# Decoder layer on one core: the feed-forward's block sums reordered, its down sums kept in PSUM, its first loads thinned, its operand stores begun by ScalarE

## The chip, the cores and the metric

One Trainium2 chip, one of its cores. The metric is device time of one execution in microseconds; the kernel before is given by the median of three runs.

## The reference

One decoder layer on a sequence of 1024 tokens of width 1024, all in 32-bit floats, cut to what matters here:

```
mod = silu(c) @ w_ada + b_ada                  # six vectors of 1024: sh1, sc1, g1, sh2, sc2, g2
h   = x * (1 + sc1) + sh1
y   = mixers(h @ w_in) @ w_o                   # sparse attention (8 heads) and gated MLP (8 groups)
x   = LN(alpha * x + (1 + g1) * y)
h   = x * (1 + sc2) + sh2
f   = (silu(h @ w1) * (h @ w3)) @ w2           # w1, w3: 1024 x 2816, w2: 2816 x 1024
out = LN(alpha * x + (1 + g2) * f)
```

## The kernel before

All matrix products of the large projections are made from split operands: a 32-bit value a becomes aH (rounded to the engine's fp32r form by ScalarE, `rnd` at L102) and aL = a − aH (by VectorE, `sub` at L107), and a product is three matmuls, HH, HL and LH, summed in PSUM. So TensorE's work needs, for every operand, one ScalarE and one VectorE operation ahead of it (`split`, L179).

The order of work on each engine comes from a list scheduler that simulates the program's time while it is built; the order in the source is the priority, and `order(a, b)` adds an edge that orders a after b without a semaphore. Tiles come from pools with a fixed number of buffers: `B` (41 of 128x1024), `RAW` (4 of 128x1024, where loads land), `H2` (4 of 128x512; with the tag "pt" another 6), and in PSUM `G` (3 banks), `OT` (1 bank) and `S2` (2 pairs of banks). Every transfer of the kernel before is started by SyncE, whose queue takes them in order.

*Start.* c is loaded as a row copied to 128 partitions (`crow`), goes through tanh to silu(c), and `mod_col` (L156) sums each row of the transposed w_ada against it. `make_h` (L228) makes the split h of a 128-row block k from x and mod; `split_start` (L197) splits the v and k weights of two blocks; `start_mm` multiplies. The loads stand in one written order (`dseq`): crow, cols, v weights, then per block the modulation weights and x.

*Turn to the feed-forward.* After the output projection (`out_proj`) VectorE makes the layer norm Z of 8 row tiles; the last ones end with L990. `make_h2a` transposes rows 512 to 1023 of Z on TensorE and makes the split h operands B11 and B21, `make_h2b` those of rows 0 to 511: B22 and the sums T1 to T4.

*Up.* The two up products (w = 0 is w1 with silu, w = 1 is w3) and the down product each use a block scheme with seven products of half-size blocks instead of eight (the Strassen-Winograd form), so every operand of it is a block or a sum of blocks. A step (p, w) covers 256 columns of the weights; there are 22. `prep1` loads and splits A11 and A12, `prep2` makes the sums S1 to S4 and A22. `up_first`, `up_second` and `up_rest` multiply (`prod`, 12 matmuls each), copy and add the seven products, and `act_out` makes silu and the product. Each block and each sum of blocks that the down product needs is stored to DRAM by `put` (L1001) at once: seven of the activations and seven of w2 for each p (`w2_sums`, scaled by g2 on POOL at L1011). The first NE = 4 steps' `up_first` and `up_second`, which need B11 and B21 alone, run while `make_h2b` works.

*Down.* For each of seven products P1 to P7 (order `DN`) and 11 blocks p, `prep_down` loads a stored operand pair (cr), splits it, and `down` makes 12 matmuls, four row tiles t by three. P1 to P7 are added to the residual rows R on VectorE (`add`, L1168), P1 and P5 by way of copies (`sn`) on ScalarE. Small pieces of work wait in `todo` and are taken one per product by `step()`. The last LAST = 6 blocks of P4 are taken row tile by row tile; after each t its layer norm follows, in `norm_slow` (VectorE, ScalarE, POOL) for t = 0 and 1, in `norm_fast` (VectorE) for t = 2 and 3.

Of the kernel before, what the change touches and what calls it, by code (L numbers as in the profile page):

```python
# [19 lines left out]
NK = 8  # L20
# [15 lines left out]
W1 = 768  # L36
# [7 lines left out]
def hymba_kernel(ctx, tc, x, c, w_ada, b_ada, w_in, cmp_pos, cmp_w1, cmp_w2, vn_g, vn_b, w_s, b_s,  # L44
# [88 lines left out]
    def dseq(o, i):  # L133
        d = dma(o, i)
        if seq[0] is not None:
# [4 lines left out]
    dseq(crow, c[0:1].to_broadcast([128, 1024]))  # L140
# [56 lines left out]
    def split_start(k2):  # L197
        h, l, t = B("wH", F32R), B("wL", F32R), B("wK", F32R)
        chain("A", A_.activation(h, wvr[k2], AF.Copy))
        chain("A", A_.activation(t[:, 0:512], wkr[k2], AF.Copy))  # L200
        chain("V", sub(l, wvr[k2], h))
        chain("V", sub(t[:, 512:1024], wkr[k2], t[:, 0:512]))
        for i in range(2):
            wv.append((h[:, i * 512:(i + 1) * 512], l[:, i * 512:(i + 1) * 512]))
# [89 lines left out]
    for k in range(NK):  # L294
        for j in (1, 0):
            chain("V", mod_col(j, j, k, adat[j, k]))
        if k == 0:
            split_start(0)
        if k % 2 and k < 7:
            split_start(k // 2 + 1)  # L300
        make_h(k, 0, 512, W1)
# [519 lines left out]
    X1, BOP = [None] * NK, {n: [None] * 4 for n in ("B11", "B21", "B22", "T1", "T2", "T3", "T4")}  # L821
# [14 lines left out]
    def make_h2a():  # L836

        for k in range(NK):
            if k % 2 == 0:
                bh, bl, bx = B("h2H", F32R), B("h2L", F32R), B("h2X")  # L840
            h, l, xx = halves(bh)[k % 2], halves(bl)[k % 2], halves(bx)[k % 2]
# [5 lines left out]
            X1[k] = xx  # L847
# [4 lines left out]
    def make_h2b():  # L852

        for i in range(4):
            if i % 2 == 0:
                bh, bl = B("h2H", F32R), B("h2L", F32R)
            xs = []
            for k in (i, 4 + i):
                p = S2("pz")[:, 0, :]
                trans4(p, lambda j: Z[j][:, k * 128:(k + 1) * 128])  # L860
                xx = H2(F32, "pt")
                affine("A", xx, p, k)
                xs.append(xx)
                if k >= 4:
                    h, l = halves(bh)[i % 2], halves(bl)[i % 2]
                    affine("A", h, p, k)
                    sub(l, xx, h)
                    BOP["B22"][i] = (h, l)
            ta, tb = B("ta"), B("tb")
            (t1, t3), (t2, t4) = halves(ta), halves(tb)  # L870
            V_.tensor_tensor(t1, xs[0], X1[i], SUB)
            V_.tensor_tensor(t3, xs[1], xs[0], SUB)
            V_.tensor_tensor(t2, xs[1], t1, SUB)
            V_.tensor_tensor(t4, X1[4 + i], t2, SUB)
            for t, (n0, n1) in ((tb, ("T2", "T4")), (ta, ("T1", "T3"))):
                h, l = split(t)
                for n, hh, ll in zip((n0, n1), halves(h), halves(l)):
                    BOP[n][i] = (hh, ll)
            yield
        spill_z(0)  # L880

# [86 lines left out]
    for n_, (ts, chunks) in enumerate(groups):  # L968
# [13 lines left out]
        for t, o in zip(ts, os_):  # L982
# [7 lines left out]
            V_.tensor_scalar(z, z, mv[:, 0:1], mv[:, 2:3], SUB, MULT)  # L990
# [7 lines left out]
    DN = ("P1", "P5", "P2", "P3", "P6", "P7", "P4")  # L998
    comb = {(i, p): dram.tile([128, 1024], F32, name=f"comb{i}_{p}") for i in DN for p in range(NP)}

    def put(i, p, side, src):  # L1001

        dma(comb[i, p][:, side * 512:side * 512 + 512], src)

    def w2_sums(p):
        (b11, b12), (b21, b22) = r = [halves(RAW("w2r")) for _ in range(2)]
        for z in range(2):
            load(r[z][0], w2[(2 * p + z) * 128:(2 * p + z + 1) * 128, 0:512], 8)
            load(r[z][1], w2[(2 * p + z) * 128:(2 * p + z + 1) * 128, 512:1024], 8)
            for a in range(2):  # L1010
                P_.tensor_tensor(r[z][a], r[z][a], rowt["g2r"][:, a * 512:a * 512 + 512], MULT)  # L1011
# [27 lines left out]
    def prep2(p, w):  # L1039
# [6 lines left out]
        V_.tensor_tensor(s1, a21, a22, ADD)  # L1046
# [312 lines left out]
```

## Time and profile before

| | |
|---|---|
| runs | 1258.51 us median of 3 (1256.99 to 1259.09) |
| the profiled execution's own time | 1261.56 us |
| its span, first to last instruction | 1259.8 us |
| busy: TensorE, VectorE, ScalarE, POOL | 95%, 77%, 46%, 28% |
| mean granted clock of TensorE | 0.988 |
| DMA, mean | 150 GB/s, 188.59 MB |

Times in the profile count from the first instruction. PE is TensorE, PEld its weight loads, DVE VectorE, ACT ScalarE, POOL GpSimd, SP or SPq SyncE and its queue. A matmul's busy time is longer than its place in a full pipeline, so for the pace of TensorE the reader counts matmuls in a stretch. The idle time before an instruction is given with what ended it. Names are those of the program's tiles without their numbers; combP is the DRAM buffer of the down operands.

### The profile page before, as it was taken

Reading aid. Unit: us, or ns where it says so; the run is one execution under the profiler, and the core shown is the slowest. Engines: PE = TensorE matmul, PEld = TensorE weight load, DVE = VectorE, ACT = ScalarE, POOL = GpSimd, SP = SyncE. Lnnn points to the kernel's source line nnn. Section 1 sums busy time; section 2 is a strip of 40 time slices with the busy share of each in tenths; the row PEclk is TensorE's granted clock in tenths of the full one; section 3 lists DMA queues with packets and bytes.
Section 4 is the critical chain, followed back from the end, with each engine's and each line's share of the span. In section 5 each row is a group of like instructions: output and inputs, shape, how many; then the busy total and the mean of one; then the engine's idle time right before and its main releaser. Section 6 shows DMA issues by size and latency. Waiting matters only on the chain. (4 is left out here: it accounts for less than half of the span.)

```text
span 1259.8 us, 16940 instructions
## 1 busy us (share of the span) xinstructions
PE 1196.9 (95%) x5880; PEld 994.4 (79%) x5880; DVE 964.6 (77%) x1686; ACT 581.2 (46%) x1065; POOL 355.8 (28%) x357
## 2 busy tenths in 40 slices
PE   5999999999999999998899999999999989999994
PEld 4888888788888888887678777888878868888873
DVE  6568798699999998778858668666686758784587
ACT  5653223499889994134433232332333325454131
POOL 0022035166456753103133222332313310000123
PEclk9999999999999999999999999999999999999997
DMA  9623549110000006634245555556555479686252
GB/s 353 250 61 120 162 127 246 45 68 1 2 1 2 2 18 219 200 113 147 84 141 188 175 172 176 176 161 198 181 179 181 161 264 331 220 300 213 77 191 83
DMA packets 131225, 188.59 MB, mean 150 GB/s; under 512 B 16834, under 2 KB 77378, under 8 KB 131140
## 3 DMA queue, kind: packets, MB, share of 16 engines
q1 hardware_dynamic: 131140, 187.52, 45.6%
q8 instruction: 46, 0.75, 0.3%
q14 instruction: 39, 0.32, 0.1%
HBM read 136.63 MB, written 48.76 MB: 147 GB/s over the span
## 5 line engine op out<-in xcount | busy, mean ns | idle before, releaser
L730 POOL TENSOR_SCALAR P<-P,ast,gate 128x640 f32<-128x640 f32 (+7 forms) x128 | 99.6, 784 | 66.7 <-DVE ast L729 49.7
L107 DVE TENSOR_TENSOR wL<-cr,wH 128x1024 fp32r<-128x1024 f32 x77 | 99.9, 1317 | 22.9 <-ACT wH L102 22.4
L102 ACT ACTIVATE wH<-cr 128x1024 fp32r<-128x1024 f32 x77 | 79.8, 1058 | 70.0 <-DMA cr<-combP 65.8
L1011 POOL TENSOR_TENSOR w2r<-w2r,g2r 128x512 f32<-128x512 f32 x44 | 61.5, 1414 | 168.3 <-DMA w2r<-in_w 80.2
L107 DVE TENSOR_TENSOR pt<-pt,pt 128x512 fp32r<-128x512 f32 (+1 forms) x148 | 99.8, 682 | 7.0 <-ACT pt L102 6.3
L663 ACT ACTIVATE P<-P,ast 128x640 f32<-128x640 f32 (+7 forms) x128 | 93.8, 734 | 2.0 <-DVE ast L662 1.5
L102 ACT ACTIVATE pt<-pt 128x512 fp32r<-128x512 f32 (+1 forms) x148 | 87.2, 592 | 16.2 <-PE pt L128 13.6
L1122 POOL TENSOR_TENSOR pt<-pt,pt 128x512 f32<-128x512 f32 x22 | 34.7, 1576 | 165.5 <-ACT pt L1121 156.6
L128 PE MATMUL pt<-ident,P 128*128 128x128 f32 x528 | 79.0, 272 | 0.2 <-DVE pt L107 0.2
L1077 DVE TENSOR_TENSOR h<-h,pt 128x512 f32<-128x512 f32 x33 | 26.3, 798 | 64.3 <-POOL pt L1124 63.9
L128 PEld LDWEIGHTS pt<-ident,P 128*128 128x128 f32 x528 | 65.0, 140 | 12.9 <-issue 0.5
L1065 PE MATMUL pcd<-wH,wH 128*128 128x512 f32 x176 | 69.9, 399 | 5.1 <-ACT pt L1116 2.9
L1229 PE MATMUL py<-wH 128*128 128x512 f32 x176 | 68.6, 394 | 2.5 <-DVE r L1168 2.5
L1067 PE MATMUL pa<-h2H,wL 128*128 128x512 f32 x176 | 69.0, 392 | 1.6 <-DVE wL L107 1.6
L1065 PE MATMUL pa<-h2H,wH 128*128 128x512 f32 x176 | 69.3, 395 | 0.6 <-ACT h L1074 0.2
L1066 PE MATMUL pcd<-wL,wH 128*128 128x512 f32 x176 | 69.5, 395 | 0.0
L1067 PE MATMUL pcd<-wH,wL 128*128 128x512 f32 x176 | 69.1, 393 | 0.0
L1229 PE MATMUL py<-wH,wL 128*128 128x512 f32 x176 | 69.0, 393 | 0.0
L1229 PE MATMUL py<-wL,wH 128*128 128x512 f32 x176 | 68.9, 392 | 0.0
L1066 PE MATMUL pa<-h2L,wH 128*128 128x512 f32 x176 | 68.8, 391 | 0.0
L102 ACT ACTIVATE wH<-raw 128x1024 fp32r<-128x1024 f32 (+2 forms) x41 | 42.4, 1041 | 56.0 <-DMA combP<-wt 21.1
L107 DVE TENSOR_TENSOR wL<-raw,wH 128x1024 fp32r<-128x1024 f32 (+2 forms) x41 | 49.0, 1199 | 18.0 <-ACT wH L102 16.2
(299 smaller groups left out, 3590.8 us busy)
## 6 DMA issues: line engine op xcount, KB each, us to landing
cr<-combP SPq DMA_DIRECT2D x77, 512.0 KB, 4.7
raw<-in_w SPq DMA_DIRECT2D x48, 512.0 KB, 5.6
ada<-in_w_adaT SPq DMA_DIRECT2D x32, 512.0 KB, 8.1
w2r<-in_w SPq DMA_DIRECT2D x44, 256.0 KB, 3.0
combP<-wt SPq DMA_DIRECT2D x44, 256.0 KB, 3.6
combP<-as SPq DMA_DIRECT2D x44, 256.0 KB, 2.2
combP<-w2r SPq DMA_DIRECT2D x33, 256.0 KB, 2.1
combP<-h SPq DMA_DIRECT2D x33, 256.0 KB, 3.1
```

Of the source, the lines that this page charges most:

```text
L102: A_.activation(o, i, AF.Copy)
L107: return V_.tensor_tensor(o, i, f(h), SUB)
L128: nc.tensor.transpose(out=p[:, j * 128:(j + 1) * 128], in_=src(j), identity=ident)
L663: A_.activation(P, P, AF.Exp, scale=-1.0, bias=nm, accum_out=den)
L730: P_.tensor_scalar(P, P, st[:, 2, hh:hh + 1], gcol(i, h, br), MULT, MULT)
L1011: P_.tensor_tensor(r[z][a], r[z][a], rowt["g2r"][:, a * 512:a * 512 + 512], MULT)
L1065: nc.tensor.matmul(o, lh, rh, start=start and i == 0, stop=False, skip_group_check=not start)
L1066: nc.tensor.matmul(o, lh, rl, start=False, stop=False, skip_group_check=not start)
L1067: r = nc.tensor.matmul(o, ll, rh, start=False, stop=i == 3, skip_group_check=not start)
L1077: V_.tensor_tensor(s, s, c, MULT)
L1122: P_.tensor_tensor(p5, p5, p7, ADD)
L1229: lastm[0] = nc.tensor.matmul(o, x_[:, ts_], y_[:, 512:1024], start=not cont and p == 0 and n == 0, stop=p == NP - 1 and n == 2, skip_grou ...
```

## The change

c is loaded as one row and spread over the partitions by two matmuls against ones; the first v weights are loaded after the first modulation weights and x, and the k weights of a block are split apart from the v weights. `make_h2b` works on full tiles of 1024 columns and finishes its operands in the order T1 with B22, T2, T3, T4; `prep2` of the first two steps is ordered behind the last layer norm and behind make_h2b's last sum; NE is 5. In `up_rest` POOL makes one sum and VectorE adds the product d from PSUM; the first step takes S1·T1 and S4·B22 before S2·T2. The stores of `put` are begun by ScalarE. Three down operands are prepared before the last up step. P6, P7 and P4 go on in P1's banks, P3 in P5's, and the copies `sn` fall away. LAST is 7, and every row tile at the end goes through `norm_fast`.

```diff
-    dseq(crow, c[0:1].to_broadcast([128, 1024]))
+    dseq(crow[0:1], c[0:1])
...
+    pcr = S2("pcr")
+    for a in range(2):
+        nc.tensor.matmul(pcr[:, a, :], ones[0:1], crow[0:1, a * 512:a * 512 + 512], start=True, stop=True)
+    pcr = pcr.rearrange("p a n -> p (a n)")
     th = B("th")
-    A_.activation(th, crow, AF.Tanh, scale=0.5)
-    V_.scalar_tensor_tensor(crow, th, 1.0, crow, ADD, MULT)
+    A_.activation(th, pcr, AF.Tanh, scale=0.5)
+    V_.scalar_tensor_tensor(crow, th, 1.0, pcr, ADD, MULT)
...
-    load_wv(0)
     for k in range(NK):
...
         load_x(k, 0, W1)
         if k == 0:
+            load_wv(0)
             load_wkc(0)
...
     def make_h2b():
 
+        x12, x22, x11, x21 = [], [], X1P[0:2], X1P[2:4]
         for i in range(4):
...
+            if i % 2:
+                sub(bl, x22[-1], bh)
+                BOP["B22"][i - 1:i + 1] = zip(halves(bh), halves(bl))
+                t1 = x11[i // 2]
+                V_.tensor_tensor(t1, x12[-1], t1, SUB)
+                h, l = split(t1)
+                BOP["T1"][i - 1:i + 1] = zip(halves(h), halves(l))
             yield
         spill_z(0)
+
+        def place(n, j, t):
+            h, l = split(t)
+            lasth[:] = lasts
+            BOP[n][2 * j:2 * j + 2] = zip(halves(h), halves(l))
+        for j in range(2):
+            V_.tensor_tensor(x11[j], x22[j], x11[j], SUB)
+            V_.tensor_tensor(x21[j], x21[j], x11[j], SUB)
+            place("T2", j, x11[j])
+            yield
+        for j in range(2):
+            V_.tensor_tensor(x12[j], x22[j], x12[j], SUB)
+            place("T3", j, x12[j])
+            yield
+        for j in range(2):
+            place("T4", j, x21[j])
+            yield
...
-            V_.tensor_scalar(z, z, mv[:, 0:1], mv[:, 2:3], SUB, MULT)
+            lastz = V_.tensor_scalar(z, z, mv[:, 0:1], mv[:, 2:3], SUB, MULT)
...
-    DN = ("P1", "P5", "P2", "P3", "P6", "P7", "P4")
+    DN = ("P1", "P5", "P6", "P3", "P2", "P7", "P4")
...
-        dma(comb[i, p][:, side * 512:side * 512 + 512], src)
+        A_.dma_start(comb[i, p][:, side * 512:side * 512 + 512], src)
...
-                P_.tensor_tensor(r[z][a], r[z][a], rowt["g2r"][:, a * 512:a * 512 + 512], MULT)
+                order(P_.tensor_tensor(r[z][a], r[z][a], rowt["g2r"][:, a * 512:a * 512 + 512], MULT), lasth[0])
...
-    def up_rest(p, w, a):
+    def up_rest(p, w, a, c_first=False):
...
         prod(c, o["S1"], BOP["T1"])
         p5 = H2(F32, "pt")
         A_.activation(p5, c, AF.Copy)
+        if c_first:
+            third()
+            second()
+        P_.tensor_tensor(p5, p5, p1, ADD)
         if a is not None:
             up_second(p, w, a)
         prod(d, o["S3"], BOP["T3"])
+        V_.tensor_tensor(p5, p5, d, ADD)
+        act_out(p, w, 3, p5)
+        if not c_first:
+            third()
         p7 = H2(F32, "pt")
-        A_.activation(p7, d, AF.Copy)
-        P_.tensor_tensor(p5, p5, p7, ADD)
-        prod(c, o["S4"], BOP["B22"], False)
-        P_.tensor_tensor(p5, p5, p1, ADD)
-        act_out(p, w, 3, p5)
...
-    NE = 4
+    NE = 5
     for n in range(NE):
         prep1(*steps[n])
-    prep2(*steps[0])
-    prep2(*steps[1])
+    prep2(*steps[0], lastz)
     for n in range(NE):
         up_second(*steps[n], up_first(*steps[n]))
-        advance_h2()
+        if n == 1:
+            advance_h2(4)
     advance_h2(100)
+    prep2(*steps[1], lasth[0])
...
+    def down_start():
+        prep_to(3)
...
+        if n == len(steps) - 1:
+            down_start()
-        up_rest(*s, up_first(*s) if n >= NE else None)
+        up_rest(*s, up_first(*s) if n >= NE else None, n == 0)
...
-    LA2, LAST = 4, 6
+    LA2, LAST = 4, 7
...
-            cont = i in ("P2", "P3", "P4")
+            cont = i not in ("P1", "P5", "P2")
...
-            o = bX if i in ("P1", "P2", "P6") else bY
+            o = bY if i in ("P5", "P3", "P2") else bX
...
-            elif i == "P3":
-                add(c12, o[t])
...
+            add({"P1": c11, "P5": c22, "P6": c12, "P3": c12, "P2": c11, "P7": c22}[i], o[t])
...
     for t in range(4):
         for p in range(NP - LAST, NP):
-            down("P4", p, t, o[t], True)
-        add(R[t][:, HS[0]], o[t])
-        if t < 2:
-            for _ in norm_slow(t):
-                pass
-        else:
-            norm_fast(t)
+            down("P4", p, t, bX[t], True)
+        chain("V", V_.tensor_tensor(R[t][:, HS[0]], R[t][:, HS[0]], bX[t], ADD))
+        norm_fast(t, HS[::-1] if t == 3 else [slice(0, 1024)])
```

## Rows read from the trace of the kernel before

**Rows 1.** The page, part 1: busy us (share of the span) x instructions

```profile
PE 1196.9 (95%) x5880; PEld 994.4 (79%) x5880; DVE 964.6 (77%) x1686; ACT 581.2 (46%) x1065; POOL 355.8 (28%) x357
```

**Rows 2.** Stretches: length; busy us (x count) by engine; granted clock, DMA, GB/s

```profile
0.00:14.20 14.20, 0.00 (x0) 0.00 (x0) 6.27 (x13) 4.86 (x7) 0.68 (x6) 1.00 0.87 297
14.20:21.00 6.80, 6.78 (x23) 5.47 (x24) 5.25 (x9) 5.25 (x9) 0.00 (x0) 1.00 1.03 402
580.00:645.00 65.00, 54.09 (x230) 41.49 (x229) 47.51 (x65) 28.76 (x39) 17.81 (x12) 0.95 0.36 118
645.00:1015.00 370.00, 364.57 (x1587) 297.68 (x1587) 263.65 (x327) 120.12 (x170) 105.40 (x74) 1.00 0.56 179
1015.00:1030.00 15.00, 10.61 (x40) 7.55 (x39) 9.03 (x13) 5.02 (x6) 3.84 (x3) 0.93 0.45 145
1030.00:1200.00 170.00, 170.00 (x749) 140.69 (x748) 119.34 (x120) 71.84 (x73) 7.05 (x7) 1.00 0.69 242
1205.00:1220.00 15.00, 12.46 (x49) 9.86 (x48) 12.63 (x18) 3.31 (x4) 1.06 (x3) 0.89 0.56 191
1243.50:1259.80 16.30, 0.00 (x0) 0.00 (x0) 13.25 (x14) 2.06 (x2) 6.07 (x3) 0.59 0.34 129
```

**Rows 3.** Timeline of the first 15 us: start, us, instruction [idle before]; line L411

```profile
5.27 1.06 ACT L146 ACTIVATE th<-crow 128x1024 f32<-128x1024 f32 x1 [3.21 <-DMA crow<-in_c]
...
9.80 1.28 DVE L158 CUSTOM_DVE_ANT_0 ada<-ada,crow,cols 128x1024 f32<-128x1024 f32 x1 [1.93 <-DMA ada<-in_w_adaT]
...
12.84 0.63 ACT L200 ACTIVATE wK<-pt 128x512 fp32r<-128x512 f32 x1 [3.29 <-DMA pt<-in_w_in]
...
13.37 1.29 ACT L232 ACTIVATE hH<-x,mod 128x512 fp32r<-128x512 f32 x2
...
L411 PE MATMUL pr<-acc,ones x8: 592/592/592, 181.0 to 525.4; 128*128 128x512 f32 x8
```

**Rows 4.** VectorE's timeline, 571 to 590, and one group of 572 to 622

```profile
571.57 1.29 DVE L987 TENSOR_TENSOR h<-pwo,g1r 128x512 f32<-128x512 f32 x2 [0.33 <-PE pwo L96]
...
572.77 1.22 DVE L107 TENSOR_TENSOR wL<-sb,wH 128x1024 fp32r<-128x1024 f32 x1
...
588.15 0.68 DVE L107 TENSOR_TENSOR w<-raw,w 128x512 fp32r<-128x512 f32 x1
...
588.75 0.80 DVE L990 TENSOR_SCALAR z<-z,mv 128x1024 f32<-128x1024 f32 x1
...
L107 DVE TENSOR_TENSOR wL<-tb,wH 128x1024 fp32r<-128x1024 f32 x4 | 4.9, 1224 | 2.6 <-ACT wH L102 2.6
```

**Rows 5.** POOL and VectorE groups, up steps: busy, mean | idle before

```profile
L1122 POOL TENSOR_TENSOR pt<-pt,pt 128x512 f32<-128x512 f32 x20 | 31.6, 1578 | 127.2 <-ACT pt L1121 118.3 <-DVE wL L107 8.8
...
L1011 POOL TENSOR_TENSOR w2r<-w2r,g2r 128x512 f32<-128x512 f32 x36 | 48.2, 1354 | 141.1 <-DMA w2r<-in_w 72.7 <-ACT pt L1121 53.3 <-DVE wL L107 14.9
...
L1077 DVE TENSOR_TENSOR h<-h,pt 128x512 f32<-128x512 f32 x29 | 23.6, 813 | 50.8 <-POOL pt L1124 50.5
...
L1129 DVE TENSOR_TENSOR pt<-pt,pcd 128x512 f32<-128x512 f32 x20 | 13.6, 682 | 5.6 <-PE pcd L1067 5.6
```

**Rows 6.** Stores of L1003, ns min/median/max; what SyncE waited for, 640 to 1020

```profile
L1003 SPq DMA_DIRECT2D combP<-wt x44: 319/320/2416, 620.6 to 1008.3; - x44
...
SPq L1003 <- POOL w2r L1011: 39.6, 24, 3.9
```

**Rows 7.** VectorE's splits at the turn to down; TensorE's waits, 1015 to 1245

```profile
1027.11 5.46 DVE L107 TENSOR_TENSOR wL<-cr,wH 128x1024 fp32r<-128x1024 f32 x4
...
PE px L1229 <- DVE wL L107: 2.1, 1, 2.1
...
PE py L1229 <- DVE r L1168: 2.5, 1, 2.5
```

**Rows 8.** Timeline after the last matmul

```profile
1247.14 3.49 DVE L1213 SCALAR_TENSOR_TENSOR zo<-zo,stb,l 128x512 f32<-128x512 f32 x2
...
1255.39 1.40 DVE L1213 SCALAR_TENSOR_TENSOR zo<-zo,stb,l 128x512 f32<-128x512 f32 x2
```

More of the change, by code (lines that the diff above doesn't have):

```diff
@@ L864, in make_h2b @@
                 if k >= 4:
[L865 to L878, printed above, removed]
+                    affine("A", halves(bh)[i % 2], p, k)
+            if i % 2:
[5 more added lines that the diff above has]
+                BOP["T1"][i - 1:i + 1] = zip(halves(h), halves(l))
@@ L1068, in prod, with room @@
         marks.append(r)
+    early_acts = []
+    def room(p, q):
+        if q or (p, 0) not in steps[:NE]:
+            return H2()
+        if not early_acts:
+            early_acts.extend(halves(B("ea")))
+        return early_acts.pop(0)
     def act_out(p, w, q, c):
         if w == 0:
-            s = silu[p, q] = H2()
+            s = silu[p, q] = room(p, q)
             A_.activation(s, c, AF.Silu)
@@ L1132, in hymba_kernel, with prep_down, prep_to @@
     steps = [(p, w) for p in range(NP) for w in range(2)]
-    NE = 4
+    NE = 5
     for n in range(NE):
         prep1(*steps[n])
-    prep2(*steps[0])
-    prep2(*steps[1])
+    prep2(*steps[0], lastz)
     for n in range(NE):
         up_second(*steps[n], up_first(*steps[n]))
-        advance_h2()
+        if n == 1:
+            advance_h2(4)
     advance_h2(100)
+    prep2(*steps[1], lasth[0])
+    seq2 = [(i, p) for i in DN for p in range(NP)]
+    ops2 = {}
+    def prep_down(n):
+        if n < len(seq2):
+            raw = RAW("cr")
+            dma(raw, comb[seq2[n]])
+            ops2[seq2[n]] = split(raw)
+    LA2, LAST = 4, 7
+    done = 0
+    def prep_to(n):
+        nonlocal done
+        while done < n:
+            prep_down(done)
+            done += 1
+    def down_start():
+        prep_to(3)
     for n, s in enumerate(steps):
@@ L1228, in down @@
         for n, (x_, y_) in enumerate(((h, h), (h, l), (l, h))):
+            before = lastm[0]
             lastm[0] = nc.tensor.matmul(o, x_[:, ts_], y_[:, 512:1024], start=not cont and p == 0 and n == 0,
                                         stop=p == NP - 1 and n == 2, skip_group_check=cont)
-    def small():
-        return [h for _ in range(2) for h in halves(B("sn"))]
+            if i == "P4" and p >= NP - LAST:
+                order(lastm[0], before)
     todo = []
@@ L1278, in hymba_kernel @@
             continue
-        if i in ("P1", "P5"):
-            sn = small()
-            for t in range(4):
-                A_.activation(sn[t], o[t], AF.Copy)
-            if i == "P1":
-                p1s = sn
-                for t in range(4):
-                    later(residual(t), one(R[t][:, HS[0]], sn[t]), one(R[t][:, HS[1]], sn[t]), one(R[4 + t][:, HS[1]], sn[t]))
-            else:
-                for t in range(4):
-                    later(one(R[t][:, HS[1]], sn[t]))
+        while i == "P2" and todo:
+            step()
         for t in range(4):
             (c11, c12), (c21, c22) = halves(R[4 + t]), halves(R[t])
-            if i == "P2":
-                add(c11, o[t])
-            elif i == "P3":
-                add(c12, o[t])
-            elif i == "P7":
-                add(c22, o[t])
+            add({"P1": c11, "P5": c22, "P6": c12, "P3": c12, "P2": c11, "P7": c22}[i], o[t])
         if i == "P3":
```

117 lines of the change are left out of this document (59 added, 58 removed).

## Prediction

> **What bounds the kernel now.** I read the page first: TensorE is busy 95% of the span [rows 1]. Busy time alone hides how well it is fed, so I next read the table of stretches and counted matmuls. In 1030 to 1200 us the engine takes 749 of them in 170.00 us, 0.227 us each, at granted clock 1.00 and without a pause [rows 2]: that is the pace of a fed TensorE here, and its work is the same before and after the change (two small matmuls are added). So only time in which TensorE falls behind this pace can be won. The other rows of that table give it, count times 0.227 us taken from the length of the stretch. At the start, 14.2 us pass before the first matmul, and 23 matmuls in the next 6.8 us fall 1.6 us short. From 580 to 645 there are 230 matmuls; 32 of them are 128-column transposes, which I count at no more than 0.227 us too, so at least 65 − 52.2 = 12.8 us are lost. From 645 to 1015: 370 − 1587 × 0.227 = 9.8 us. From 1015 to 1030: 15 − 9.1 = 5.9 us. From 1205 to 1220: 15 − 11.1 = 3.9 us. After the last matmul, 16.3 us. Some 64 us in all. The three stretches with pauses show granted clocks of 0.95, 0.93 and 0.89: after a pause the clock stood at its lower level, 1.2 GHz, for a while, and that is inside the losses.
>
> **The change, part by part, each against one of these losses.**
>
> *Start.* Now the c row, copied to 128 partitions, is the first load (512 KB) and the v weights come before the modulation weights. tanh starts at 5.27 us, when crow has landed, and with its 1.06 and a product of 1.2 crow is ready at 7.5; yet the first modulation sum starts only at 9.80, held by its load, and the second v/k split at 12.84, held by another, just ahead of the first activation of h [rows 3]. After: crow is one row, spread by two 512-column matmuls against ones. Such a matmul takes 0.59 us at full clock [rows 3]; one row lands sooner than 512 KB, so I let the pair end at about 5.1 us, and crow is ready at 7.4, as before. The two modulation loads no longer stand behind 1 MB of crow and v weights, so the sums run 7.4 to 10.0 (two of 1.28), the first activation of h (0.65) ends at 10.7 and no longer stands behind the wK split. First matmul at about 11.0: 3.2 us won. Ends: 1.5 (the spread row comes 1.7 us late at the lower clock) and 4.5 (the second modulation load was what counted).
>
> *Into the feed-forward, 580 to 645.* This stretch is VectorE's. The last layer norm's operations run from 571.57 to 589.55 us [rows 4], and between them stand nine splits and block sums of prep2(0) and prep2(1), the first and last of which are shown: at 1.22 or 0.68 us each some 8 us. The change orders prep2's first sums behind lastz, so lastz comes at about 582, 7 us sooner (all times here on the clock of the kernel before; the start's gain shifts them). make_h2b's VectorE work itself hardly shrinks: now 8 splits of 1.22 us (four of them are a row of [rows 4]) and 20 half-width operations of 0.68, 23.4 us; after, 8 splits of 1.22, 8 full-width sums and subtractions at the same price and 2 for B22, all 1024 wide, 22 us. But now all four operand pairs of T1 to T4 are finished together, and after they come in the order in which the first step uses them: T1 and B22 after 7.4 us, T2, T3, T4 after 7.4, 4.9 and 2.4 more. On VectorE: 582, prep2(0) 5.8, T1 ready at 595, T2 603, T3 608, T4 611, then prep2(1) with up_rest(0)'s own sums until about 621, its first split at 618. On TensorE: five early steps of 24 matmuls instead of four (27.2 us) from 572.7, 32 transposes (3.5), then S1·T1, S4·B22, S2·T2, S3·T3, A22·T4 at 2.7 us each: 603.4, 608.9, 611.6, 614.3, 617. Only the next step then waits 1 to 2 us for prep2(1). With a lower clock after that pause I leave 4 of 12.8 us: 9 won. Ends: 2 (VectorE has as much to do as before, and prep2(0) now stands behind lastz) and 12.
>
> *Steady up steps, 645 to 1015, and the stores.* Per step POOL makes two sums in a row (1.58 us and about as much again), and VectorE, which takes its queue in order, stands 50.8 us in front of the product that needs the second [rows 5]; POOL in turn has four 1.35 us scalings of w2 per pair of steps in the same queue [rows 5]. After, POOL makes only p5 + p1, for which the copy of c is ready 5.4 us before S3·T3 ends, and VectorE adds d from PSUM for 0.68 us, the price of the like sum at L1129 [rows 5]. ScalarE loses a copy a step, VectorE gains 0.68 us: hidden, VectorE being 263.65 of 370 us busy [rows 2]. Hiding fails if POOL's sum is later than the 2.7 us that S4·B22 gives; then A22·T4 is late next, by what is over. I credit half of the 9.8 us, 5.
>
> Against it stands the move of the 154 stores to ScalarE. On SyncE each takes 0.32 us to issue [rows 6], 49 us for all, 2.2 us a step, and the queue waits for their sources: for the scaled w2 blocks alone 24 times, 39.6 us, at the longest 3.9 [rows 6]. No row shows a store on ScalarE. From below: ScalarE is busy 120 of 370 us [rows 2], the scheduler puts the stores where their sources should be done, and the loads for weights and w2 now pass no store on SyncE: nothing lost, up to 3 gained. From above: behind a waiting store stand, in ScalarE's order, the copies of c and of a from PSUM and the splits of weights; TensorE waits for them as soon as the store is later than the 2.7 us of one product. I take 2 us lost, near the lower end, because the waits average 1.65 us, under that cover. Net for the stretch: 3 won; ends 8 won and 30 lost.
>
> What the move itself can give, a rule of the Trainium skill bounds further ("DMA: Bandwidth & Descriptors", Issuing engines are not separate DMA queues): transfers from several queues share the same DMA engines, and starting them elsewhere saves only the sequencer's time to start them. By it the move gives nothing here beyond SyncE's 49 us, of which TensorE feels little; without the 2 us I charge, the sum would be 2 us better, not more.
>
> *Up to down, 1015 to 1030.* At the end VectorE splits the first four down operands only from 1027.11 on, in 5.46 us, behind the last step's sums, and TensorE waits for them, 2.1 us the longest time [rows 7]. After, three operands are loaded and split before the last step's products. Of 5.9 us lost I leave 1.4 (the last POOL sum): 4.5 won, ends 3 and 5.5.
>
> *Down.* The block sums stay in PSUM: eight copies and eight additions of half width fall away on engines that were not the bound. P4 still follows P7 in the same banks, where TensorE now waits 2.5 us for the addition that reads them [rows 7]; P2 after P3 is a second such place. Each bank's addition (0.69) fits in the three matmuls of the next one (0.68) if VectorE comes at once, and after the change it has less queued. Of 3.9 us I leave 0.9 for both places: 3 won; ends 3 lost and 4 won.
>
> *Tail.* Now the last matmul is followed by 16.3 us [rows 2]: VectorE still has the products of two slow rows and the fast row of t=2 to do; its two halves at L1213 take 3.49 us beside POOL's additions, against 1.40 for the next pair alone [rows 8]. After, every row is fast, in one chain: per t 21 matmuls, 4.8 us, against 0.69 + 0.69 + 0.35 + 2 × 1.25 = 4.2 us on VectorE, so it keeps up. After the last matmul: add 0.69, statistics 1.0, four halves 2.8 (0.70 each [rows 8]), and from the last VectorE result at 1256.79 to the span's end 3.0 [rows 8]: 7.7 us. 8.5 won; ends 6.5 and 9.
>
> **Sum.** 3.2 + 9 + 3 + 4.5 + 3 + 8.5 = 31.2 us. The profiled execution took 1261.6 us, so 1230.4 by its own time; it lies 3.1 us over the median of the runs, and the forecast for the median is 1227 us.
>
> **Rivals.** *The stores stall ScalarE (other side).* Place: a store in ScalarE's queue whose source VectorE or POOL has not finished, with the PSUM copy or a weight split behind it. For: SyncE's waits of up to 3.9 us [rows 6] plus three issues, 4.9 us, exceed one product's cover by 2.2. Against: ScalarE's low share. It decides from 31.2 / 22 = 1.4 us a step on; at 2.0 a step the time is 1271, at 0.7 a step 1242. The Trainium skill ("TensorE: Matmul & The Clock Gate", the specification table) calls ScalarE's queue a strict first-in-first-out of 8 entries, which is this rival's mechanism; the sum by it would be 1242 to 1271, and no row of the kernel before has a ScalarE store to tell.
>
> *VectorE still sets the way in.* Work there is 22 us against 23.4, prep2(0) moves behind lastz, and five kept first products leave one of the six pt buffers for the first step's p5 and p7, one after the other. Then 2 instead of 9 are won: 1234.
>
> *All covers hold.* The losses at 580 to 1030 fall to 3 us, the stores cost nothing: 11 us more than my sum, 1216.
>
> **Chances.** My forecast 0.43, VectorE rival 0.16, all covers 0.14, stores stall partly 0.16, wholly 0.11. Faster by more than 0.2% (2.5 us, about what a measurement here tells from no change): 0.43 + 0.16 + 0.14 + 0.14 = 0.87; same 0.03; slower 0.10. The range 1214 to 1247 leaves out the full stall and the last tenth of the others.
>
> **What would show it.** Right: first matmul near 11 us; lastz about 20 us before the first T1 product, and at most one pause of TensorE over 1 us between 580 and 645; VectorE's wait for POOL in the up steps under 15 us; no pause of TensorE over 1 us between the last up and the first down product; 7 to 8 us after the last matmul. Wrong: pauses of TensorE that end with ScalarE's copies or splits, ScalarE itself idle in front of stores; or 580 to 645 as sparse as now.

## The result, and the profile after

The changed kernel is slower: 1275.51 us (median of 4 runs, 1274.86 to 1278.86) against 1258.03 for the kernel before (median of 4), a ratio of 1.0129 with a 95% interval of 1.011 to 1.0148. The forecast was 1227, its range 1214 to 1247. The profiled execution has a span of 1277.1 us. First its page, part 1 (busy time, share of the span, instructions):

```profile
PE 1208.2 (95%) x5884; PEld 1000.7 (78%) x5884; DVE 969.0 (76%) x1682; ACT 564.6 (44%) x1033; POOL 324.8 (25%) x331
```

As in [rows 1], TensorE is busy 95% of a span that is now 17 us longer. The table of stretches, in the columns of [rows 2], shows where it fell behind:

```profile
0.00:11.60 11.60, 3.75 (x4) 1.16 (x4) 5.06 (x12) 4.12 (x5) 0.68 (x6) 1.00 0.81 278
11.60:21.00 9.40, 9.08 (x29) 7.25 (x30) 8.11 (x13) 6.46 (x11) 0.00 (x0) 1.00 1.03 399
580.00:645.00 65.00, 52.33 (x209) 40.94 (x208) 47.31 (x48) 30.22 (x40) 10.76 (x6) 0.87 0.31 101
645.00:1015.00 370.00, 349.12 (x1499) 283.34 (x1499) 265.90 (x331) 104.52 (x142) 86.21 (x59) 0.98 0.53 172
```

From 580 to 645 TensorE takes 209 matmuls where it took 230, and from 645 to 1015 it takes 1499 where it took 1587 [rows 2]. At the prediction's pace of 0.227 us the missing 21 and 88 are 4.8 and 20.0 us. The same can be read over the whole program: both kernels have 5880 records of matmuls apart from those that spread crow (two matmuls, four records), so the start of the n-th one, counted from 0, less its start in the kernel before says how far a kernel is behind (+) or ahead (−). Worked out from the records of the profiled executions, us:

```
n-th matmul                   3064   3246   3337    4901    4958    5879   end of
(its start in the one before)  570    620    645    1010    1028    1243   span
the change                    -1.6   -7.5   +3.3   +24.5   +19.1   +26.1   +17.3
e1  stores on SyncE           +0.8   -5.6   +4.4    +6.9    +2.2   +11.3    +2.5
e2  before, stores on ScalarE +1.7   +5.6   +4.4   +19.7   +20.0   +18.5   +18.5
e7  e1, shift on VectorE      -1.4   -8.0   +1.4    +2.4    -3.1    -3.4   -12.3
e9  e1, two tiles              0.0   -6.8   -3.3    -3.0    -8.4    -2.4   -11.2
k1  change, sum on VectorE    -2.8  -10.7   -7.0   +17.3   +11.9   +19.8   +11.0
k2  change, two tiles         -1.5   -8.0   -5.1    -8.0   -13.4    -8.0   -16.8
g1  three edits               -2.0   -8.9   +0.6    -2.8    -8.2   -11.6   -20.4
g2  four edits                -2.4   -9.4    0.0    -6.6   -12.1   -15.5   -24.3
h2  g2, stores on ScalarE     -1.6   -8.6   +3.8    -5.2   -10.6   -13.9   -22.8
h1  g2, four early steps      -2.2   -5.1   -4.9   -12.4   -17.8   -21.0   -29.7
```

The lower lines belong to the experiments below. One execution is read here, and in code that the changed kernels share such a figure can move by some 3 us (from −2.8 to +0.8 at matmul 3064). The profiled execution of e1 was also the slowest of its ten, 1264.06 us against a median of 1258.22, so its line stands too high. In the line of the change, the way into the feed-forward wins 6 us up to matmul 3246 and gives 10.8 back within the next 91. The up steps lose 21 more, the turn to down wins 5.4, down loses 7, and the tail wins 8.8. Three places thus carry the miss, and each shows in the traces of the change.

*The up steps.* ScalarE's timeline in the middle of them; a row ends with the idle time before it and its releaser, and ACTq rows are DMAs that ScalarE starts:

```profile
847.44 1.58 ACTq L1027 DMA_DIRECT2D combP<-w2r  x2
849.12 0.60 ACT L1138 ACTIVATE pt<-pa 128x512 f32<-128x512 f32 x1 [10.08 <-POOL w2r L1035]
849.73 0.60 ACT L1161 ACTIVATE pt<-pcd 128x512 f32<-128x512 f32 x1
...
864.09 3.30 ACTq L1027 DMA_DIRECT2D combP<-wt  x4
869.59 1.06 ACT L102 ACTIVATE wH<-raw 128x1024 fp32r<-128x1024 f32 x1 [6.96 <-DMA combP<-wt]
```

A store costs ScalarE 0.33 us to start; what is dear is its wait. Stores of scaled w2 blocks stand in its queue until POOL has scaled them, and the copies of a and c out of PSUM stand behind, ScalarE idle for 10.08 us. The next splits then come late, the one at 869.59 after 6.96 us of idle time that ends with the store of the w2 sums, and TensorE waits for them: its own rows from 640 to 1015 are led by `pa L1093 <- ACT wH L102`, 9.5 us in 7 times. After such a pause its clock stands at the lower level, 1.2 GHz, for a while: from 910 to 920 us, after TensorE has stood 2.96 us up to 912.13, the granted clock is 0.66 and 22 matmuls fit, what is left of the pause included, where 45 or 46 fit at 1.00.

*The way in.* POOL's timeline, then VectorE's, then TensorE's, at the first up step's products:

```profile
619.02 2.13 POOL L1165 TENSOR_TENSOR pt<-pt,pt 128x512 f32<-128x512 f32 x1 [39.89 <-DVE pt L1153]
621.11 6.84 POOL L1035 TENSOR_TENSOR w2r<-w2r,g2r 128x512 f32<-128x512 f32 x4
```

```profile
618.79 3.44 DVE L107 TENSOR_TENSOR wL<-h2X,wH 128x1024 fp32r<-128x1024 f32 x2
622.15 1.74 DVE L1070 TENSOR_TENSOR sa<-raw 128x512 f32<-128x512 f32 x1
623.82 0.67 DVE L1169 TENSOR_TENSOR pt<-pt,pcd 128x512 f32<-128x512 f32 x1
624.42 1.16 DVE L1073 TENSOR_TENSOR sa<-sa,raw 128x512 f32<-128x512 f32 x1
625.50 0.67 DVE L1174 TENSOR_TENSOR pt<-pt,pcd 128x512 f32<-128x512 f32 x1
626.76 2.27 DVE L107 TENSOR_TENSOR wL<-sa,wH 128x1024 fp32r<-128x1024 f32 x1 [0.59 <-ACT wH L102]
```

```profile
626.23 0.80 PE L1093 MATMUL pcd<-wH,w 128*128 128x512 f32 x1 [5.58 <-DVE pt L1174]
```

TensorE's product A22·T4, which goes into d, starts only when L1174 has read c. The two are banks of one PSUM tile, and a product into one waits for the reader of the other. VectorE is late, and its operations beside POOL's take longer: two splits that take 2.4 us alone take 3.44, sums of 0.69 take 1.74 and 1.16, a split of 1.22 takes 2.27, 3.7 us more in all. The two operations that read one operand from PSUM keep their 0.67. Whether this slowness is what the way in loses by is asked again below, with g1 and g3.

*Down.* VectorE's, POOL's and TensorE's timelines where P4 follows P7:

```profile
1227.42 1.23 DVE L1272 TENSOR_TENSOR zo<-zo,l 128x1024 f32<-128x1024 f32 x1 [2.30 <-ACT zo L1270]
1228.56 5.65 DVE L107 TENSOR_TENSOR wL<-cr,wH 128x1024 fp32r<-128x1024 f32 x3
1234.13 1.27 DVE L1239 TENSOR_TENSOR r<-r,px 128x512 f32<-128x512 f32 x2
```

```profile
1228.79 3.19 POOL L1274 TENSOR_TENSOR zo<-zo,l 128x1024 f32<-128x1024 f32 x1 [2.69 <-DVE zo L1272]
```

```profile
1235.55 0.77 PE L1292 MATMUL px<-wH 128*128 128x512 f32 x1 [6.72 <-DVE r L1239]
```

The last product into P7's banks starts at 1228.44, and the addition that has to read them stands in VectorE's queue behind three splits. By their single records the second, which starts while POOL shifts a finished row, takes 3.38 us, the other two 1.22 and 1.21. TensorE waits 6.72 us where it waited 2.5 [rows 7].

### The profile page after: what moved, and what is told of

It is laid out like the page before. It is cut to its first block, busy times and chain, and to the rows that moved or that the text cites. A ratio compares the mean times of both kernels' runs of the same rounds, so it can differ in the third digit from the quotient of the medians.

```text
span 1277.1 us, 16839 instructions
## 1 busy us (share of the span) xinstructions
PE 1208.2 (95%) x5884; PEld 1000.7 (78%) x5884; DVE 969.0 (76%) x1682; ACT 564.6 (44%) x1033; POOL 324.8 (25%) x331
## 5 line engine op out<-in xcount | busy, mean ns | idle before, releaser
L102 ACT ACTIVATE wH<-cr 128x1024 fp32r<-128x1024 f32 x77 | 80.8, 1059 | 101.7 <-DMA cr<-combP 82.7
L102 ACT ACTIVATE pt<-pt 128x512 fp32r<-128x512 f32 (+1 forms) x148 | 87.3, 592 | 16.1 <-PE pt L128 13.5
L1093 PE MATMUL pa<-h2H,wH 128*128 128x512 f32 x176 | 72.2, 411 | 15.6 <-ACT wH L102 9.5
L102 ACT ACTIVATE wH<-raw 128x1024 fp32r<-128x1024 f32 (+2 forms) x41 | 42.4, 1041 | 79.6 <-DMA combP<-wt 43.0
L1292 PE MATMUL px<-wH 128*128 128x512 f32 x176 | 68.5, 396 | 9.1 <-DVE r L1239 6.7
L1093 PE MATMUL pcd<-wH,wH 128*128 128x512 f32 x176 | 69.8, 397 | 2.9 <-ACT pt L1161 1.8
L1292 PE MATMUL px<-wL,wH 128*128 128x512 f32 x176 | 69.2, 393 | 0.0
L1292 PE MATMUL px<-wH,wL 128*128 128x512 f32 x176 | 69.0, 392 | 0.0
L773 PE MATMUL ot<-pt,V 128*128 128x512 f32 x132 | 59.7, 452 | 0.0
```

Of the source, the lines that this page charges most:

```text
L102: A_.activation(o, i, AF.Copy)
L773: nc.tensor.matmul(ot, vs, hl[0], start=False, stop=False)
L1093: nc.tensor.matmul(o, lh, rh, start=start and i == 0, stop=False, skip_group_check=not start)
L1292: lastm[0] = nc.tensor.matmul(o, x_[:, ts_], y_[:, 512:1024], start=not cont and p == 0 and n == 0, stop=p == NP - 1 and n == 2, skip_grou ...
```

## Experiments

Each ratio is to the kernel before, with its 95% interval.

**Whose loss are the stores?** Theory A said that the stores in ScalarE's queue cost more than all the rest wins; rival B, that the rest itself starves the up steps.

```diff
 e1  (changed kernel; all stores back on SyncE)
-        A_.dma_start(comb[i, p][:, side * 512:side * 512 + 512], src)
+        dma(comb[i, p][:, side * 512:side * 512 + 512], src)
 e2  (kernel before; all stores on ScalarE)
-        dma(comb[i, p][:, side * 512:side * 512 + 512], src)
+        A_.dma_start(comb[i, p][:, side * 512:side * 512 + 512], src)
 e3  (changed kernel; the w2 blocks' stores on SyncE)
-        A_.dma_start(comb[i, p][:, side * 512:side * 512 + 512], src)
+        (dma if side else A_.dma_start)(comb[i, p][:, side * 512:side * 512 + 512], src)
 e4  (changed kernel; the other way round)
-        A_.dma_start(comb[i, p][:, side * 512:side * 512 + 512], src)
+        (A_.dma_start if side else dma)(comb[i, p][:, side * 512:side * 512 + 512], src)
```

> The whole change, but the operand stores are begun by SyncE again. Theory A (stores in ScalarE's queue stand in front of the copies of a and c and of the weight splits): the pauses of TensorE that end with ScalarE's copy of a (5.9 us) and its splits (16 us) go, and with them most of the up steps' 57 us of lost time; 1235 to 1242 us. Rival B (the reordered sums, the fifth early step and the ordering edges starve the up steps, stores or no stores): 1265 to 1276 us.

> The kernel before with nothing changed but the operand stores, begun by ScalarE. Theory A: 25 to 45 us slower than before, 1283 to 1303. Rival B: within 5 us of before, 1253 to 1263.

> The whole change, but the stores of the w2 blocks (7 of each 14) are begun by SyncE, those of the activations by ScalarE. Theory A, in the form that the waits for POOL's scaled blocks are what holds ScalarE: near the kernel with all stores on SyncE, within 6 us of it. If any store on ScalarE costs alike: half way, about 1256. Rival B: 1270.

> The whole change, but the stores of the activations (7 of each 14) are begun by SyncE, those of the w2 blocks by ScalarE. Theory A in the POOL form: still slow, 1262 to 1275. If any store costs alike: half way, about 1256. Rival B: 1270.

e1 took 1258.22 us, 0.9983 (0.997 to 0.9996); e2 1275.8, 1.0127 (1.0104 to 1.0151); e3 1256.84, 0.9974 (0.9958 to 0.999); e4 1269.57, 1.0071 (1.0049 to 1.0093). The move alone costs 1.3% on the kernel before, 15 or 16 us where A had said 25 to 45, and about as much on the changed one. It is the w2 blocks' stores that cost: with these on SyncE (e3) nothing of the loss is left. By themselves on ScalarE (e4) they cost 11 of the 17 us, so the activations' stores, which cost nothing alone, add to it there. So A was right about the place. But e1 lies 16 us or more above A's figure: nearly all the gain that the rest of the change was to bring is missing too, and B was right in that much. The next runs start from e1.

**Where does the rest go?** Four edits, one each.

```diff
 e5  (e1; the first step's p5 in a tile of its own)
-        p5 = H2(F32, "pt")
+        p5 = halves(B("ep"))[0] if c_first else H2(F32, "pt")
 e9  (e1; c and d in two PSUM tiles)
-        cd = S2("pcd")
-        c, d = cd[:, 0, :], cd[:, 1, :]
+        c, d = S2("pc")[:, 0, :], S2("pd")[:, 0, :]
 e7  (e1; the shift of finished rows on VectorE)
-        at(P_.tensor_tensor(z, z, l2[1], ADD))
+        at(V_.tensor_tensor(z, z, l2[1], ADD))
 e8  (e1; down operands further ahead only from P4 on)
-        prep_to(n + LA2 + max(0, min(4, (n - 40) // 6)))
+        prep_to(n + LA2 + max(0, min(4, n - 66)))
```

> The changed kernel with all stores on SyncE (e1_stores_sync, 1258.2 us), and the first step's p5 in a tile of its own instead of one of the six pt buffers. Theory C (the same-tile wait: S3 T3 and A22 T4 share a tile with c, so each waits for VectorE's read of the other bank): the 5.75 us pause at 621 us stays, 1257 to 1259. Rival D (the buffers: p7 can't be taken before p5 is read out): the pause falls under 3 us and the time to 1253 to 1255.

> The changed kernel with all stores on SyncE (1258.2 us), c and d of a step in two PSUM tiles, no longer two banks of one tile. Theory C (same-tile wait): the pause at 621 us falls from 5.75 us to under 3, pauses of 1 us at 660, 677 and 695 go too, 1251 to 1255 us. Rival E (VectorE's backlog of splits sets the way in, the tile is no matter): pauses move but the stretch 600 to 700 loses as much as now, 26 us, and the time is 1257 to 1259.

> The changed kernel with all stores on SyncE (1258.2 us), with the shift of a finished row (the addition of l2[1]) on VectorE, 1.28 us, no longer on POOL. Theory F (a weight split beside POOL's 3.2 us addition takes 3.3 us, not 1.2, and holds up the additions that P4 waits for): the pause of 6.95 us between P7 and P4 falls to 4 to 5 us, the time to 1255 to 1256. Rival G (VectorE's order, three splits ahead of the additions, whatever one takes): the pause stays over 6 us, 1258 to 1260 with VectorE's added work.

> The changed kernel with all stores on SyncE (1258.2 us); the down operands are fetched at most four products ahead until P7 is done, and only then up to eight. Theory G (splits of operands far ahead stand before the additions in VectorE's queue): the pause between P7 and P4 falls from 6.95 to 2 to 3.5 us, time 1253 to 1255. Rival F (POOL beside a split): two of the splits still stand there, one of them slow, pause 5 us or more, 1256 to 1258.

e5 took 1253.74 us, 0.9949 (0.9931 to 0.9966); e9 1247.76, 0.9912 (0.9878 to 0.9947); e7 1249.42, 0.9919 (0.9894 to 0.9943); e8 1257.26, 0.9982 (0.9964 to 1.0001). The shared tile and POOL's shift cost the most, both more than theories C and F said; e5, for the buffers that the prediction had as a rival, half as much. But e5 changes more than a buffer: POOL's first four scalings move from 622 us (e1) to 587, the pause in front of A22·T4 is gone, and another of 6.2 us stands earlier, for a split of the operands of S2·T2:

```profile
619.67 0.79 PE L1093 MATMUL pb<-wH,wH 128*128 128x512 f32 x1 [6.18 <-ACT wH L102]
```

In e8 the pause between P7 and P4 stays at 6.8 us, so the depth of the lookahead is not its cause. In e7 it is gone. VectorE's and TensorE's timelines of e7 at that place:

```profile
1203.99 1.23 DVE L1272 TENSOR_TENSOR zo<-zo,l 128x1024 f32<-128x1024 f32 x1 [2.31 <-ACT zo L1270]
1205.13 1.22 DVE L107 TENSOR_TENSOR wL<-cr,wH 128x1024 fp32r<-128x1024 f32 x1
1206.27 1.28 DVE L1239 TENSOR_TENSOR r<-r,px 128x512 f32<-128x512 f32 x2
```

```profile
1207.69 0.47 PE L1292 MATMUL px<-wH 128*128 128x512 f32 x1 [0.22 <-DVE r L1239]
```

The split takes 1.22 us again, and one stands before the additions, not three: with POOL out of it VectorE's queue is also ordered otherwise. Of the 6.5 us by which the pause shrinks, two splits fewer are 2.4 by these rows, and the slowness beside POOL was 2.2 (3.38 for a split of 1.22); the rest isn't accounted for, and no run took the two apart.

**Do the gains add, and what is POOL's part?** Each of g2 to g4 is g1 with one edit.

```diff
 g1  = e5 + e7 + e9
 g2  (p5 + p1 on VectorE)
-        P_.tensor_tensor(p5, p5, p1, ADD)
+        V_.tensor_tensor(p5, p5, p1, ADD)
 g3  (first w2 blocks scaled without waiting for the last up operand)
-                order(P_.tensor_tensor(r[z][a], ...), lasth[0])
+                P_.tensor_tensor(r[z][a], ...)
 g4  (the second step's operands early)
     prep2(*steps[0], lastz)
+    prep2(*steps[1], lastz)
...
-    prep2(*steps[1], lasth[0])
```

> The changed kernel with all stores on SyncE (1258.2 us) with three changes at once: c and d in two PSUM tiles (alone 9 us better by the ratios to before), p5 of the first step in a tile of its own (alone 4 us), the last norm's shift on VectorE (alone 8 us). If the three are separate losses: 1236 to 1239 us. If the first two lift one and the same pause at 600 to 640: 1240 to 1243.

> As g1_three_mended, and p5 + p1 on VectorE in every step, no longer on POOL. Theory H (an operation of VectorE on two SBUF operands that starts beside one of POOL's takes up to 1.8 us instead of 0.69, so POOL's sums cost VectorE as much as they save): 1 to 4 us faster than g1. Rival I (VectorE has no room for 22 more sums of 0.68 us, 15 us): 2 to 5 us slower than g1.

> As g1_three_mended, with POOL's scaling of the first w2 blocks free of its place behind the last up operand, as in the kernel before. Theory H (POOL beside VectorE): the four scalings now fall in the stretch before 620 us or stay away from the first step's sums; the pause near 620 falls by 1 to 2 us, 1 to 3 us faster than g1. Rival J (they only move the collision on to the operands T1 to T4): same within 1 us, or 1 to 3 slower.

> As g1_three_mended, with the operands of the second up step (prep2(1)) free to be made behind the last layer norm, as in the kernel before, not behind the last of T1 to T4. Theory K (the order behind T4 makes the second step late): pauses between 620 and 665 fall by 3 to 5 us, those before 620 rise by 1 to 2, 2 to 4 us faster than g1. Rival E (VectorE's backlog as a whole sets the way in): the pauses only move forward, within 1 us of g1 or slower by up to 4.

g1 took 1241.21 us, 0.9839 (0.9824 to 0.9853); g2 1235.88, 0.9797 (0.9783 to 0.9812); g3 1240.29, 0.9829 (0.9812 to 0.9845); g4 1249.2, 0.9903 (0.9886 to 0.9921). The three gains add up but for 3 or 4 us, as they would if two of them lift one pause. In g2 it went as theory H has it, and by a little more: VectorE does 22 more sums and the kernel is 5 us faster. g4 is 8 us slower, more than rival E allowed: TensorE stands 9.9 us up to 598, so here it was right to put the second step's operands behind T1 to T4, and theory K falls.

g3 is no different, but it tests nothing: in g1 POOL makes the first four scalings at 587 already, long before the first step's sums, and g3 makes them at 588. g1's POOL:

```profile
587.20 2.56 POOL L1035 TENSOR_TENSOR w2r<-w2r,g2r 128x512 f32<-128x512 f32 x2 [8.53 <-DMA w2r<-in_w]
590.39 2.54 POOL L1035 TENSOR_TENSOR w2r<-w2r,g2r 128x512 f32<-128x512 f32 x2 [0.64 <-issue]
```

VectorE's sums of the way in take 0.69 us again in g1, and still g1 loses 9.5 us from matmul 3246 to 3337, while k2 below, with the scalings at 620 as in the change, loses 2.9. So POOL's neighbourhood alone does not decide there. In g1 TensorE stands 4.3 us for the copy of c and 3.7 for a split; what sets the way in stays open.

**What is still open.**

```diff
 h1  (g2; four early steps, p5 back among the pt buffers)
-    NE = 5
+    NE = 4
-        p5 = halves(B("ep"))[0] if c_first else H2(F32, "pt")
+        p5 = H2(F32, "pt")
 h2  (g2; stores on ScalarE, as in the change)
 h3  (kernel before; c and d in two tiles)
```

> As g2_c_sum_vector (1235.9 us), with four early up steps as in the kernel before, no longer five, and p5 of the first step back among the six pt buffers. Theory L (the fifth early step takes 10 tiles and a kept product that the first steps then lack): the pause of 4.6 us for the copy of c goes, its cover of 5.4 us too; within 2 us of g2 or up to 4 faster. Rival M (a fifth step is 5.4 us of cover for VectorE, and VectorE sets the way in): 3 to 6 us slower than g2.

> As g2_c_sum_vector, with the stores begun by ScalarE, as in the change. Theory A (a store in ScalarE's queue holds the copies and splits behind it while its source waits for POOL or a load): 10 to 18 us slower than g2, 1246 to 1254, with pauses in the up steps that end with ScalarE. Rival N (the stall came from VectorE's late sums beside POOL, which are mended here): under 6 us slower.

> The kernel before, with c and d of a step in two PSUM tiles, and nothing else of the change. Theory C (the same-tile wait costs the up steps of the kernel before too): the 12 us lost from 640 to 1020 fall by 4 to 8, 1250 to 1254 us. Rival: with POOL's two sums in a row VectorE reads d late anyway and the wait is the chain's, not the tile's: 1256 to 1259.

h1 took 1232.68 us, 0.978 (0.9766 to 0.9795); h2 1238.21, 0.9825 (0.981 to 0.9839); h3 1257.14, 0.9969 (0.9958 to 0.9981). The fifth early step and its buffers lose 2 to 3 us more than they cover (theory L). In the kernel before the shared tile costs 0.3%, under what theory C asked for. h2 was the surprise: with g2's edits the same 154 stores on ScalarE cost 0.3%, not 1.3, and the table has all of it in the way in (+3.8 against 0.0 at matmul 3337). Theory O, a circle through POOL's sum, was made for that, and the last three runs took the edits apart.

```diff
 k1  (changed kernel, stores on ScalarE; p5 + p1 on VectorE, as in g2)
 k2  (changed kernel, stores on ScalarE; c and d in two tiles, as in e9)
 k3  (e1, stores on SyncE; p5 + p1 on VectorE)
```

> The changed kernel (1275.5 us), stores on ScalarE, with p5 + p1 on VectorE in every step, no longer on POOL. Theory O (a circle: POOL's sum beside VectorE slows the block sums, so raw buffers come free late, w2 loads late, POOL scales them late, and the store that waits for the scaling holds up ScalarE's copies, on which POOL's next sum waits): 1258 to 1265 us, the pauses of the up steps mostly gone. Theory A (a store in ScalarE's queue costs by itself): 1270 to 1276, as the sums alone gave 5 us in g2.

> The changed kernel (1275.5 us), stores on ScalarE, with c and d of a step in two PSUM tiles. Theory O: the circle stays, and only the 9 us that the same edit gave with the stores on SyncE are won, or fewer: 1266 to 1270. If late TensorE steps, not POOL, feed the circle: below 1262.

> The changed kernel with all stores on SyncE (1258.2 us) and p5 + p1 on VectorE. Theory H (POOL beside VectorE) as in g2: 4 to 6 us faster, 1252 to 1254; with k1 it closes the square of the two edits: theory O makes k1 and k3 differ by under 7 us, theory A by 15 or more.

k1 took 1272.25 us, 1.0099 (1.007 to 1.0128); k2 1244.79, 0.9901 (0.9884 to 0.9918); k3 1257.16, 0.9991 (0.9976 to 1.0006). Theory O falls: with POOL's sum away the stores cost 15 us still (k3 to k1), as theory A has it while the tile is shared. Theory H is narrowed too, since k3 is no faster than e1: the sum on VectorE pays only where the tiles are apart (g2). And two PSUM tiles, with the stores still on ScalarE, win 31 us (29 by the ratios): far under 1262, the bound of the expectation's second case, in which late steps of TensorE feed the circle. Put as a square, four kernels one edit apart:

| | stores on SyncE | stores on ScalarE |
|---|---|---|
| c and d in one tile | 1258.22, 0.9983 (e1) | 1275.51, 1.0129 (the change) |
| c and d in two tiles | 1247.76, 0.9912 (e9) | 1244.79, 0.9901 (k2) |

The stores cost 17 us with the shared tile and, within the intervals, nothing without it. g2 and h2, also with two tiles, agree but for 2 to 4 us; e2, e4 and k1, all with one tile, pay 11 to 16. The groups of ScalarE's rows from 640 to 1015 show what differs; the figure behind the bar's second stroke is its idle time before them. First the change:

```profile
L102 ACT ACTIVATE wH<-raw 128x1024 fp32r<-128x1024 f32 x17 | 18.0, 1060 | 69.0 <-DMA combP<-wt 43.0 <-DVE as L1122 9.8 <-DVE pt L1174 7.3
...
L1138 ACT ACTIVATE pt<-pa 128x512 f32<-128x512 f32 x16 | 9.4, 590 | 72.4 <-POOL w2r L1035 55.1 <-DMA combP<-w2r 8.7 <-PE pcd L1095 8.5
```

k1, still slow:

```profile
L1138 ACT ACTIVATE pt<-pa 128x512 f32<-128x512 f32 x16 | 9.4, 589 | 67.6 <-POOL w2r L1035 49.6 <-DVE pt L1174 9.4 <-PE pcd L1095 8.7
```

k2:

```profile
L102 ACT ACTIVATE wH<-raw 128x1024 fp32r<-128x1024 f32 x17 | 17.9, 1055 | 72.2 <-DVE as L1122 26.2 <-PE pb L1095 10.3 <-DMA combP<-h 9.3
...
L1138 ACT ACTIVATE pt<-pa 128x512 f32<-128x512 f32 x17 | 10.0, 590 | 12.0 <-DVE as L1124 5.0 <-POOL w2r L1035 2.8 <-DMA combP<-w2r 1.6
```

In front of the copy of a, ScalarE idles 72.4 us in the change, 67.6 in k1 and 12.0 in k2. In the change and in k1 three stores of scaled blocks stand straight ahead of that copy in the last eight pairs of steps (seven in k1). In the last seven pairs of k2, and of h2, two of them stand ahead of a weight split and one ahead of the copy, as k2's timeline shows:

```profile
830.00 0.33 ACTq L1027 DMA_DIRECT2D combP<-w2r  x1
830.42 0.90 ACTq L1027 DMA_DIRECT2D combP<-as  x2
831.43 0.60 ACT L1138 ACTIVATE pt<-pa 128x512 f32<-128x512 f32 x1 [1.44 <-PE pc L1094]
```

So the stores' price is not theirs alone: it goes with the shared tile. How, is not shown. The two tiles change the written order of ScalarE's queue along with the waits, and the order alone doesn't explain it: in e2 two of the stores stand ahead of a weight split too, ScalarE idles 8.7 us there as in k2, and TensorE still pauses 1.4 to 3.1 us four times from 700 us on, where k2 has none over 0.6. Of the 31 us 9 or 10 come with the stores on SyncE too (e1 to e9). Other single edits move orders as well: in k1 and k3 POOL's first scalings stand at 587, as in e5. Nor is it settled why the splits' idle time behind the w2 sums' stores, which e1 has as well (63.6 us), reaches TensorE in the change and hardly in e1.

## Why the prediction was wrong, term by term

Two steps failed most: the cover that made the stores' charge 2 us, where they cost 17, and the credits for the way in, POOL's sums and down, none of which e1 shows.

- *Sum.* The rival "the stores stall ScalarE", taken wholly, gave 1271, and its mechanism is in the trace; but the measured 1275.5 isn't that case alone, and that the two figures lie close is luck. The stores cost 17 us (e1; 15 by e2), 0.8 a step, nearer the partial case's 0.7 than the full one's 2.0, and of the 33.2 us that the rest was to win (the sum without the 2 charged for stores) e1 has 2.
- *Stores, 2 us charged.* This step failed in its choice: "near the lower end, because the waits average 1.65 us, under that cover". That average is of waits on SyncE [rows 6], with loads behind them and no copy or split. In ScalarE's queue three stores come one after another, for blocks that POOL scales one after another, and the wait ahead of one copy is up to 10.1 us, not 3.9. That alone doesn't make the price: with c and d in two tiles the stores cost nothing (e9 to k2), so the cover that the prediction counts on seems to hold when the tile is parted and fails when it is shared; by which wait it is lost stays open. The stretch's lower end, 30 lost, held: it lost 21. The Trainium skill ("DMA: Bandwidth & Descriptors", Issuing engines are not separate DMA queues) bounds what such a move can save, not what it can cost, and by e2 the move saved nothing here.
- *POOL's sums, 5 us credited.* The wait went as forecast: VectorE's idle time in front of POOL's results falls from 50.8 us [rows 5] to 1.2. But it brought nothing while c and d share a tile: with the stores on SyncE the up steps from matmul 3337 to 4901 lose 2.5 us against before in e1 and 1.0 in e7. VectorE now waits for TensorE instead. In kernels with two tiles the stretch wins 3.4 us (g1), and with p5 + p1 on VectorE 6.6 (g2), over the 5 credited; which part of that is the wait for POOL was not separated. That S4·B22 gives 2.7 us of cover failed too: c and d share a tile, and S4·B22 waits for the reader of d (in e1 L1169 ends at 697.10 and S4·B22 starts at 697.15).
- *Way in, 9 us.* The first part came: the last layer norm ends at 579.98 us, not 589.55, and 5.9 us are won up to matmul 3246. The step that failed is "only the next step then waits 1 to 2 us": the first step waits 5.6 for its own sums, and the next 3.8 for prep2(1)'s split. VectorE's work was counted at each operation's price alone, while POOL's first four scalings now run beside it (6.84 us from 621.11); but g1, without that, loses as much there, so this isn't shown to be the cause. The loss of 10.8 is 3 or 4 with c and d in two tiles (e9, k2), over 9 again with p5 in a tile of its own besides (g1, g2), and 0.2 without that tile and with four early steps (h1), so the buffers that the rival named are part of it, in a way that no run took apart. h1 has 2.7 us of the 9.
- *Down, 3 us.* The step "if VectorE comes at once, and after the change it has less queued" failed: 7 us lost, outside the bound of 3. With the shift off POOL (e7) down wins 0.3 us, and in h1 3.2.
- *Start, 3.2 us.* Right in kind, mis-sized: the row is there at 2.42 us, but the two matmuls that spread it are four records and take 3.75 us; the 0.59 of [rows 3] is the price of a record, half a matmul (L411 runs four matmuls in its eight records). So tanh starts at 6.21 us, not 5.1, the first matmul at 11.92, and in the next 9.4 us TensorE falls 2.8 short, where 1.6 was lost before; 1.4 us are left.
- *Turn to down, 4.5, and tail, 8.5.* Right: 5.4 and 8.8. Between the up and the down products TensorE waits 0.8 us. In the tail the last matmul starts at 1269.21 and the span ends 7.9 us later, forecast 7.7. VectorE's rows after it:

```profile
1269.63 0.69 DVE L1365 TENSOR_TENSOR r<-r,px 128x512 f32<-128x512 f32 x1 [1.06 <-PE px L1292]
...
1272.72 1.41 DVE L1284 SCALAR_TENSOR_TENSOR zo<-zo,stb,l 128x512 f32<-128x512 f32 x2
```

Of the signs for right, three came: VectorE's wait for POOL, the turn to down, the tail. Between 580 and 645 us TensorE pauses twice for over 1 us (5.58 and 3.77), not once, and both signs for wrong came.

h1, which keeps most of the change but has its stores on SyncE, two tiles, four early steps and two sums off POOL, wins 2.2%, where 2.5% were forecast: most of the gain was there to be had, by another kernel.

## What to carry to other kernels

Price a DMA start that is moved into a computing engine's queue by the wait for its source and by what stands behind it there, not by its issue time or the average wait on the queue that it comes from, and ask whether TensorE has the slack to bear that wait: the same stores cost 17 us here or nothing. Before crediting a wait that goes away, look for the engine that will wait next; the 50 us wait for POOL was worth nothing as long as the tile was shared. A PSUM tile of two banks joins the readers of one to the writers of the other in this program: parting them won 9 to 31 us in the changed kernels and 4 in the kernel before. And before reading a single edit as a single cause under a scheduler, compare the order of the engines' work in both traces: g3's edit changed none that mattered, e5's more than it meant to.

## What the runs showed of the hardware

An operation of VectorE that reads two SBUF operands and starts while one of POOL's runs is held up. Counted in the change's records from 571 to 1015 us, sums of 128x512 with both operands in SBUF take 0.69 us when no sum or scaling of POOL runs beside them (159) and also when POOL's begins during them (21), but 1.64 in the mean and 1.82 at most when they begin during POOL's (33); those with an operand in PSUM keep 0.69 in every case (92). So `h<-h,pt` (L1115) takes 1.02 us in the mean in the up steps, while `pt<-pt,pcd` (L1174), with one operand in PSUM, takes 0.69. The rows, VectorE's groups from 640 to 1015:

```profile
L1115 DVE TENSOR_TENSOR h<-h,pt 128x512 f32<-128x512 f32 x29 | 29.7, 1024 | 0.3
L1174 DVE TENSOR_TENSOR pt<-pt,pcd 128x512 f32<-128x512 f32 x19 | 13.1, 687 | 49.1 <-PE pcd L1095 49.1
```

The Trainium skill says so ("SBUF — State Buffer", SBUF: two separate sides): of a POOL operation and a VectorE operation with two SBUF inputs, whichever starts first holds a shared pair of ports for its whole instruction, and the other waits. The trace agrees by the counts above. What it costs a kernel isn't settled: moving 22 sums from POOL to VectorE won 5 us in g2 and nothing in k3.
